# A decoder step on one core: order of the mixing block, place of the first squares, gates in steps, and an earlier verdict

## Chip, cores and metric
One core of one Trainium2 chip. The metric is device time in microseconds, from the start to the end of one execution; less is better.

## What is computed
One layer of a hybrid decoder for 256 prompt tokens and 8 single-token samples: a half-step SwiGLU, a mixing block, a second half-step SwiGLU, a final RMSNorm. The mixing block runs four mLSTM heads beside eight blocks of a gated short convolution.

```python
h = h + 0.5 * swiglu(rmsnorm(h, norm_ffn1), gate1, up1, down1)
h = h + mixing_block(rmsnorm(h, norm_mix), ...)
h = h + 0.5 * swiglu(rmsnorm(h, norm_ffn2), gate2, up2, down2)
y = rmsnorm(h, norm_final)
# in the mixing block
q, k, v, o, ig, fg, gb, gc, xc = split(h @ w_in)
ha = mlstm_chunkwise(q, k, v, logi, logf, C0, n0, m0)
ha = ha * rsqrt(mean(ha * ha) + EPS) * norm_mlstm * sigmoid(o)
yb = gb * (conv3(gc * xc) + conv_b)
yb = yb * rsqrt(mean(yb * yb, per group of 128) + EPS) * norm_conv
out = concat([ha, yb]) @ w_out
```

The new states C, n, m of every sample and of the prompt, and the last convolution inputs, are outputs too. D_MODEL is 2048, D_FF 5504, a head has 256 columns.

## The kernel before
Activations lie transposed: 16 blocks `h[kb]` of 128 features by 264 columns (256 prompt tokens and 8 samples), two blocks to a tile `hpair`. All weights are fp32 in memory and are used as two fp16 parts. `fetch` (L192) issues one transfer of up to 512 KB on SyncE's queue into `wraw`, ScalarE makes the high part `whi` (L178), VectorE the rest `wlo` (L186). `three` (L223) turns each 128x128 block into three matmuls: high weights by high and by low activations, low weights by high activations. A `product` (L228) runs such triples over all 16 input blocks into one of 8 PSUM banks, 48 matmuls. Six buffers of each weight tile exist; five tiles are kept ahead (`AHEAD`).

Each engine works through its instructions in the order in which the program issues them. `at(delta, fn)` (L209) puts a step on an agenda, and `tick` (L212) runs it when that many products later are reached; half ticks lie in the middle of a product. So the program's text fixes which steps stand between which weights on ScalarE and VectorE.

- **Opening.** `products4` (L249) runs the gate and up products of the first two FFN blocks, group by group of input blocks, while `ahead` (L435) loads `h`, cuts it into the parts `x` and squares it: even blocks on ScalarE, odd ones on GpSimd, which also adds all squares into `acc` (L382). Behind the four products `finish` (L384) lets TensorE sum `acc` over partitions (`column_sums`, L349), ScalarE and VectorE make 1/root from it, and then blocks 0 and 1 are scaled and activated (L409 to L422).
- **Mixing.** `MIX_ORDER` (L60) lists heads (6 products each), convolutions (3 each) and output gates (1 each). A head's steps follow over 13 ticks: scores, values, then for the samples four rounds of state loads, updates and outputs through GpSimd's queue, then the squares of its output (ScalarE, L869, tick 10.5), their addition `rs` (VectorE, L873, tick 11), the column sums (TensorE, tick 12) and the scaling (tick 13). `gate` (L957) runs at once: VectorE scales the product into `ta`, ScalarE takes the sigmoid `tb`, VectorE multiplies it into `ha`. The output products then read the convolution blocks `yb` first and the gated blocks `xa`, cut from `ha`, after them.
- **End.** The half-size arithmetic is watched: sums of each product go to `stat`, norms to `squares`. Behind the last output `judge` (L308) reduces them, TensorE sums the verdicts, and `bad` (L497) is loaded by every engine (L109). `tc.If` (L110) would run the whole step again in full fp32; it is not taken here, and every engine branches over that second program.

Of the kernel before, what the change touches and what calls it, by code (L numbers as in the profile page):

```python
# [8 lines left out]
F32 = mybir.dt.float32  # L9
# [3 lines left out]
ALU = mybir.AluOpType  # L13
# [46 lines left out]
MIX_ORDER = "h0 c0 c1 h1 c2 c3 h2 c4 c5 h3 c6 c7 o0 o1 o2 o3 o4 o5 o6 o7".split()  # L60
# [7 lines left out]
def weight_plan(a):  # L68
# [28 lines left out]
    for db in range(KB):  # L97
        add(("out", db), a["wout"][db], KB)
# [16 lines left out]
def step(ctx: ExitStack, tc: tile.TileContext, a: dict, bad=None):  # L115
# [6 lines left out]
    AHEAD = 5 if half_size else 2  # L122

# [16 lines left out]
    nc.gpsimd.dma_start(bg, a["bg"])  # L140
# [107 lines left out]

    def products4(x, ahead):  # L249
# [33 lines left out]
    if half_size:  # L283
        stat = const.tile([128, NSTAT], F32, name="stat")
        nc.gpsimd.memset(stat, 2.0 * SUMS[0])
        squares = const.tile([128, 8], F32, name="squares")
# [69 lines left out]
    class Norm:  # L356
# [5 lines left out]
        def block(self, kb, by_act=False):  # L362
            self.cut(kb)
            self.square(kb, by_act)
# [7 lines left out]
        def square(self, kb, by_act=False):  # L372
            new = self.acc is None
            sq = t264("acc", 1) if new else t264("sq")
            if by_act:
                nc.scalar.activation(sq, h[kb], AF.Square)  # L376
            else:
                nc.gpsimd.tensor_tensor(sq, h[kb], h[kb], op=ALU.mult)  # L378
# [4 lines left out]

        def finish(self, *rest, last=False):  # L384

            self.r = t264("rstd", 1)
            self.ssum = column_sums(self.acc, *rest)
# [5 lines left out]
    def ffn(layer, norm, done, start=None):  # L393
        with tc.tile_pool(name=f"act_{norm.tag}", bufs=1) as apool:
            first = True
            for half, blocks in enumerate(HALVES):
                act = {}
                for i, j in enumerate(blocks):
                    if start is not None and j < 2:
                        if j == 0:  # L400
                            ps4 = start()
                        pg, pu = ps4[2 * j : 2 * j + 2]
                    else:
                        pg = product((layer, "g", j), norm.x, range(KB))
                        pu = None
# [8 lines left out]
                    if pu is None:  # L414
                        pu = product((layer, "u", j), norm.x, range(KB))
# [19 lines left out]
    def ahead(part):  # L435
# [5 lines left out]
        for kb in range(k0, k0 + n):  # L441
            n1.block(kb, kb % 2 == 0)
# [8 lines left out]
        product=product, split=split, rsqrt=rsqrt, column_sums=column_sums, t264=t264,  # L451
        bank=bank, at=at, tick=tick, watch=watch, high=high, low=low, PART=PART, s3=s3,
# [6 lines left out]
    def done(kb):  # L459
# [4 lines left out]
        else:  # L464
            sq = t264("sq")
            nc.vector.tensor_tensor(sq, h[kb], h[kb], op=ALU.mult)
            nf.finish(sq, last=True)
            nc.scalar.activation(h[kb], h[kb], AF.Copy, scale=gain)
# [3 lines left out]
    def judge_early():  # L472
        early.append(len(stats))
        judge(stat[:, : early[0]], SUMS)

# [9 lines left out]

    if half_size:
        watch_norm(nf.ssum)
        judge(stat[:, early[0] : len(stats)], SUMS)
        judge(squares, SQUARES)
        ps = bank()[:1, :1]  # L490
        for i, v in enumerate(verdicts):
            nc.tensor.matmul(
                ps, v, ones[:, :1], start=(i == 0), stop=(i == len(verdicts) - 1)
            )
        some = const.tile([1, 1], F32, name="some")
        nc.vector.tensor_scalar(some, ps, 128.0 * len(verdicts) - 0.5, None, op0=ALU.is_lt)
        nc.vector.tensor_copy(bad, some)  # L497


def mix(tc, a, nm, n2, h, e):  # L500
# [6 lines left out]
    bank, at, tick = e["bank"], e["at"], e["tick"]  # L507
# [39 lines left out]
    nc.gpsimd.dma_start(m0, a["m0"])  # L547

    buf = mp.tile([128, 8, NS, 2], F32, name="buf")
    nc.gpsimd.dma_start(buf, a["conv0"])  # L550
# [25 lines left out]
    def gates_rows():  # L576
# [7 lines left out]
        nc.gpsimd.dma_start(drows, rows)  # L584
        nc.gpsimd.dma_start(a["m_p"], rows[:, 1, SEQ - 1 : SEQ])

    def gates_by_token():
# [17 lines left out]
        nc.gpsimd.dma_start(a["m_s"], ms)  # L605
# [480 lines left out]
```

## Time and profile before

| | us |
|---|---|
| median of 3 runs | 1876.56 (1875.29 to 1877.31) |
| the profiled execution | 1874.37 |
| its span, first to last instruction | 1872.5 |
| TensorE busy in the span | 1830.6 (98%), 16,107 instructions |
| VectorE, ScalarE, GpSimd busy | 1191.9, 859.6, 146.8 |

The mean granted TensorE clock over the span is 0.993. In the profile PE is TensorE's matmul, PEld its weight load, DVE is VectorE, ACT ScalarE, POOL GpSimd and SP SyncE; a q behind the name means the engine's instruction queue (branches, semaphores, loads of registers). A wait is put down to the instruction that released it last. Ends of matmuls are modelled, so the spacing of their starts tells more than their durations.

### The profile page before, as it was taken

What the parts mean: (1) busy time and instruction counts of PE and PEld (TensorE: products, weight loads), DVE (VectorE), ACT (ScalarE), POOL (GpSimd) and SP (SyncE); (2) the same over time, 40 slices, a digit from 0 to 9 for tenths busy, and PEclk for the clock granted to TensorE, in tenths of its full rate; (3) what the DMA queues carried; (4) which work ended last, traced back from release to release, by engine and by line L of the source; (5) the groups of instructions that cost most, each with busy time, mean ns of one, the idle gap of its engine ahead of it and who ended that gap; (6) DMA issues with size and microseconds to landing.
All of it is one profiled execution on the core that took longest, in us unless ns stands there. A gap on an engine that the chain in (4) does not pass through costs nothing.

```text
span 1872.5 us, 38560 instructions
## 1 busy us (share of the span) xinstructions
PE 1830.6 (98%) x16107; PEld 1586.8 (85%) x16107; DVE 1191.9 (64%) x1910; ACT 859.6 (46%) x1211; POOL 146.8 (8%) x219
## 2 busy tenths in 40 slices
PE   8999999999999999999999899999999999999994
PEld 6888888888888888888888688888888888888884
DVE  8666655466666557888888666666655456666453
ACT  6444443344444444656566645444443434444441
POOL 5000000000000211211211021000000000000110
PEclk9999999999999999999999999999999999999997
DMA  7666565656565555878778565656656656655551
GB/s 263 215 198 200 185 206 187 207 189 198 190 199 181 201 187 189 280 236 290 263 236 296 167 206 188 207 188 196 202 189 192 206 187 197 202 188 186 197 192 54
DMA packets 114714, 381.11 MB, mean 204 GB/s; under 512 B 14797, under 2 KB 19997, under 8 KB 114529
## 3 DMA queue, kind: packets, MB, share of 16 engines
q1 hardware_dynamic: 106048, 350.79, 57.4%
q0 software_dynamic: 8192, 27.57, 4.3%
q8 instruction: 128, 2.10, 0.4%
q14 instruction: 58, 0.47, 0.1%
q10 hardware_dynamic: 288, 0.19, 0.1%
HBM read 366.72 MB, written 11.78 MB: 202 GB/s over the span
## 4 chain that ended last, share of the span: by engine, by line
PE 82%; DVE 9%; issue 3%; ACT 2%; DMA 2%; POOL 0%; SPq 0%; DVEq 0%; ACTq 0%; POOLq 0%
PE ps L225 27%; PE ps L224 27%; PE ps L226 27%; DVE wlo L186 3%; DMA rb<-dr 1%; DVE cs L842 1%; ACT whi L178 1%; DVE jk L853 1%; ACT jk L861 1%; ACT L329 0%; DMA wraw<-in_w1gu 0%; DVE x L186 0%; DVE qkv L514 0%; DVE h L480 0%; DVE rs_q L338 0%
## 5 line engine op out<-in xcount | busy, mean ns | idle before, releaser
L186 DVE SCALAR_TENSOR_TENSOR wlo<-wraw,whi 128x1024 f16<-128x1024 f32 (+2 forms) x683 | 787.7, 1194 | 233.7 <-ACT whi L178 233.5
L226 PE MATMUL ps<-x,wlo 128*128 128x264 f16 x2752 | 759.6, 276 | 4.3 <-DVE wlo L186 4.3
L224 PE MATMUL ps<-x,whi 128*128 128x264 f16 x2752 | 759.6, 276 | 1.6 <-ACT whi L178 1.4
L225 PE MATMUL ps<-x,whi 128*128 128x264 f16 x2752 | 759.6, 276 | 0.0
L178 ACT ACTIVATE whi<-wraw 128x1024 f16<-128x1024 f32 (+2 forms) x683 | 664.9, 1016 | 165.5 <-PE ps L225 159.3
L226 PEld LDWEIGHTS <-wlo 128*128 128x128 f16 (+1 forms) x5296 | 518.6, 98 | 84.4 <-DVE wlo L186 6.5
L225 PEld LDWEIGHTS <-whi 128*128 128x128 f16 (+1 forms) x5296 | 518.6, 98 | 81.2 <-issue 1.8
L224 PEld LDWEIGHTS <-whi 128*128 128x128 f16 (+1 forms) x5296 | 518.6, 98 | 80.2 <-ACT whi L178 2.1
L224 PE MATMUL ps<-a,whi 128*128 128x264 f16 x1376 | 379.8, 276 | 0.0
L225 PE MATMUL ps<-a,whi 128*128 128x264 f16 x1376 | 379.8, 276 | 0.0
L226 PE MATMUL ps<-a,wlo 128*128 128x264 f16 x1376 | 379.8, 276 | 0.0
L224 PE MATMUL ps<-xm,whi 128*128 128x264 f16 (+1 forms) x912 | 252.3, 277 | 0.0
L225 PE MATMUL ps<-xm,whi 128*128 128x264 f16 (+1 forms) x912 | 252.3, 277 | 0.0
L226 PE MATMUL ps<-xm,wlo 128*128 128x264 f16 (+1 forms) x912 | 252.2, 276 | 0.0
L178 ACT ACTIVATE a<-tc 128x264 f16<-128x264 f32 x86 | 36.4, 423 | 295.0 <-DVE tc L418 292.6
L413 ACT ACTIVATE tb<-ta 128x264 f32<-128x264 f32 x86 | 36.3, 423 | 224.0 <-DVE ta L410 222.1
L425 DVE SCALAR_TENSOR_TENSOR h<-ps,h 128x264 f32<-128x264 f32 x64 | 27.7, 433 | 159.5 <-PE ps L226 159.5
L417 DVE TENSOR_TENSOR tc<-ps,rstd 128x264 f32<-128x264 f32 x86 | 37.1, 432 | 94.5 <-PE ps L226 94.5
L378 POOL TENSOR_TENSOR acc<-h 128x264 f32<-128x264 f32 x3 | 1.9, 626 | 1177.0 <-DVE stat L294 589.1
L410 DVE TENSOR_TENSOR ta<-ps,rstd 128x264 f32<-128x264 f32 x86 | 37.2, 432 | 60.4 <-PE ps L226 60.2
L186 DVE SCALAR_TENSOR_TENSOR a<-tc,a 128x264 f16<-128x264 f32 x86 | 37.3, 433 | 42.2 <-ACT a L178 42.2
L382 POOL TENSOR_TENSOR acc<-acc,sq 128x264 f32<-128x264 f32 x59 | 55.2, 936 | 6.4 <-ACT sq L376 1.8
(184 smaller groups left out, 864.8 us busy)
## 6 DMA issues: line engine op xcount, KB each, us to landing
wraw<-in_w2gu SPq DMA_DIRECT2D x172, 512.0 KB, 4.9
wraw<-in_w1gu SPq DMA_DIRECT2D x171, 512.0 KB, 4.8
wraw<-in_win SPq DMA_DIRECT2D x112, 512.0 KB, 5.5
wraw<-in_w1d SPq DMA_DIRECT2D x80, 448.0 KB, 4.1
wraw<-in_w2d SPq DMA_DIRECT2D x80, 448.0 KB, 4.0
wraw<-in_wout SPq DMA_DIRECT2D x32, 512.0 KB, 4.5
rb<-dr POOLq DMA_DIRECT2D x16, 513.0 KB, 10.2
wraw<-in_w1d SPq DMA_DIRECT2D x16, 512.0 KB, 4.4
```

The lines of the kernel that those rows point to most:

```text
L178: nc.scalar.activation(dst, src, AF.Copy, scale=scale)
L186: nc.vector.scalar_tensor_tensor(dst, src, scale, hi, op0=ALU.mult, op1=ALU.subtract)
L224: nc.tensor.matmul(ps, wh, xk[:, 0, :], start=first, stop=False)
L225: nc.tensor.matmul(ps, wh, xk[:, 1, :], start=False, stop=False)
L226: nc.tensor.matmul(ps, wl, xk[:, 0, :], start=False, stop=last)
L382: nc.gpsimd.tensor_tensor(self.acc, self.acc, sq, op=ALU.add)
L410: nc.vector.tensor_tensor(zg, pg, norm.r, op=ALU.mult)
L413: nc.scalar.activation(sg, zg, AF.Silu)
L417: nc.vector.tensor_tensor(zu, pu, norm.r, op=ALU.mult)
L425: nc.vector.scalar_tensor_tensor(h[db], ps, 0.5 / (sw * sa[layer]), h[db], op0=ALU.mult, op1=ALU.add)
L842: nc.vector.scalar_tensor_tensor(c[:, b, eb], rb[:, b, HD : 2 * HD], self.v[eb][:, col : col + 1], c[:, b, eb], op0=ALU.mult, op1=ALU.add,)
L853: nc.vector.tensor_tensor(jk, c, rb[:, :, :HD].unsqueeze(2).to_broadcast([128, 2, 2, HD]), op=ALU.mult)
```

## The change
- `MIX_ORDER`: head 1 follows one convolution, heads 2 and 3 two, and three convolutions stand behind the last head.
- The opening no longer squares. Behind the four products TensorE runs gate and up of block 2 as well; `square_pairs` lets ScalarE square two blocks of `h` at once, and GpSimd adds pairs, 528 columns at a time. The column sums then read both halves of the pair. Blocks 0, 1 and 2 are activated behind them.
- A gate becomes a class: sigmoid and multiplication are agenda steps one half to two ticks after its product, on a tile `zo` of its own; the cuts of `ha` are split in a high and a low step.
- `products2` runs the first two output products by turns, half of the input blocks each.
- The last norm is watched by a ScalarE activation that accumulates, the other norms are judged early, and the verdict is formed behind the sixth of the 16 last multiplications.
- In the full fp32 program (not run here) all transfers of GpSimd's queue go to SyncE's: `queue` stands for `nc.gpsimd` there and in the mixing block. In both programs `h[0]` is loaded on SyncE's queue, before the first weights.

```diff
-MIX_ORDER = "h0 c0 c1 h1 c2 c3 h2 c4 c5 h3 c6 c7 o0 o1 o2 o3 o4 o5 o6 o7".split()
+MIX_ORDER = "h0 c0 h1 c1 c2 h2 c3 c4 h3 c5 c6 c7 o0 o1 o2 o3 o4 o5 o6 o7".split()
...
+    half = KB // 2
+    for k0 in (0, half):
+        for db in range(2):
+            add(("out", db), a["wout"][db][:, k0 : k0 + half], half)
+    for db in range(2, KB):
         add(("out", db), a["wout"][db], KB)
...
+    queue = nc.gpsimd if half_size else nc.sync
...
-    nc.scalar.dma_start(h[0], a["xt"][:, 0, :])
     nc.scalar.dma_start(vecs, a["vecs"])
+    nc.sync.dma_start(h[0], a["xt"][:, 0, :])
...
+    def products2(keys, x, order):
+        ps = [bank()[:, :T] for _ in keys]
+        k = 0
+        while k < len(order):
+            tick()
+            for j, key in enumerate(keys):
...
+                if j == 0:
+                    tick(0.5)
+            k += n
+        return ps
...
+        def square_pairs(self, pool, pairs):
+            for i in pairs:
+                tag = f"sq{min(i, 1)}"
+                sq = pool.tile([128, 2, T], F32, tag=tag, name=tag, bufs=1 + 2 * min(i, 1))
+                nc.scalar.activation(sq, hpair[i], AF.Square)
+                if i == 0:
+                    self.acc = sq
+                else:
+                    nc.gpsimd.tensor_tensor(self.acc, self.acc, sq, op=ALU.add)
...
+                    if first and start is not None:
+                        ps4 = start()
+                        for n, ps in enumerate(ps4):
+                            early[n // 2, "gu"[n % 2]] = ps
+                        for step, pairs in ((0, (0, 1)), (1, (2, 3)), (1.5, (4, 5)), (2, (6, 7))):
+                            at(step, norm.square_pairs, apool, pairs)
+                        tick(0)
+                        for which in "gu":
+                            early[2, which] = product((layer, which, 2), norm.x, range(KB))
...
         for kb in range(k0, k0 + n):
-            n1.block(kb, kb % 2 == 0)
+            n1.cut(kb)
...
+            if half_size:
+                j = len(stats)
+                stats.append(j)
+                nc.scalar.activation(
+                    t264("ta"), nf.ssum, AF.Copy, scale=2.0**10, accum_out=stat[:, j : j + 1]
+                )
...
+        judge(squares, SQUARES)
...
+        if half_size and kb == 5:
+            judge_late()
...
+    class Gate:
+        def __init__(self, ob):
+            self.ob = ob
+            self.z = project(O + ob, tag="zo" if e["half_size"] else "ta")
+            steps = (1, 1.5, 2, 2) if ob == last[-1] else (1.5, 2, 2.5, 3)
+            at(steps[0], self.sigmoid)
+            at(steps[1], self.apply)
+            if ob in last:
+                at(steps[2], cut_high, ob)
+                at(steps[3], cut_low, ob)
...
-        for ob in tail:
-            gate(ob)
-            cut(ob)
...
+        for db, ps in enumerate(e["products2"]([("out", 0), ("out", 1)], x3, order)):
+            result(db, ps)
+        for db in range(2, KB):
+            result(db, product(("out", db), x3, order))
```

What the order of instructions becomes is shown at three places. First ScalarE's list in the opening, before: `x` is the high part of a block of `h`, `sq` its square.

```order
L178 ACTIVATE whi<-wraw 128x1024
L178 ACTIVATE x_423<-h_85,gains 128x264
L376 ACTIVATE sq<-h_85 128x264
L178 ACTIVATE x_429<-h_85,gains 128x264
L178 ACTIVATE whi<-wraw 128x1024 x6
L329 ACT_TABLE_LOAD
```

ScalarE's list at the same place now:

```order
L183 ACTIVATE whi<-wraw 128x1024 x6
L413 ACTIVATE sq_472<-h_78 128x528
L413 ACTIVATE sq_474<-h_79 128x528
L413 ACTIVATE sq_477<-h_80 128x528
L413 ACTIVATE sq_480<-h_81 128x528
L183 ACTIVATE whi<-wraw 128x1024
L413 ACTIVATE sq_514<-h_82 128x528
L413 ACTIVATE sq_517<-h_83 128x528
L413 ACTIVATE sq_544<-h_84 128x528
L413 ACTIVATE sq_547<-h_85 128x528
L183 ACTIVATE whi<-wraw 128x1024 x2
L356 ACT_TABLE_LOAD
```

All squares have moved behind the opening's weights, eight of 528 columns with one weight tile between them.

Second VectorE's list around the last head's addition of squares `rs`, before (`ha` is a gate's multiplication, `yc` a convolution's scaling):

```order
L945 SCALAR_TENSOR_TENSOR yc<-yc,vecs,rs 128x264
L514 TENSOR_TENSOR ta<-ps,rstd 128x264
L294 TENSOR_REDUCE stat<-ps 128x1
L962 SCALAR_TENSOR_TENSOR ha_8886<-ha_8886,vecs,tb 128x264
L873 TENSOR_TENSOR rs<-sq_13183 128x264
L186 SCALAR_TENSOR_TENSOR wlo<-wraw,whi 128x1024 x2
```

VectorE's list at the same place now:

```order
L997 SCALAR_TENSOR_TENSOR yc<-yc,vecs,rs 128x264
L566 TENSOR_TENSOR zo<-ps,rstd 128x264
L321 TENSOR_REDUCE stat<-ps 128x1
L925 TENSOR_TENSOR rs<-sq_12944 128x264
L984 TENSOR_TENSOR yc<-yc,tc 128x264
L191 SCALAR_TENSOR_TENSOR wlo<-wraw,whi 128x1024 x2
```

The multiplication of the gate whose product has just ended no longer stands ahead of the addition.

Third the end of the first program on VectorE, before (`h_78` to `h_85` are the pairs of output blocks):

```order
L480 TENSOR_TENSOR h_85<-h_85,rstd 128x264 x2
L304 TENSOR_REDUCE squares<-ps 128x1 x2
L312 TENSOR_SCALAR ok<-stat 128x9
L313 SCALAR_TENSOR_TENSOR ok<-stat,ok 128x9
L317 TENSOR_REDUCE verdict_23238<-ok 128x1
L312 TENSOR_SCALAR ok<-squares 128x8
L313 SCALAR_TENSOR_TENSOR ok<-squares,ok 128x8
L317 TENSOR_REDUCE verdict_23243<-ok 128x1
L496 TENSOR_SCALAR some<-ps 1x1
L497 CAST bad<-some 1x1
```

VectorE's end now:

```order
L543 TENSOR_TENSOR h_80<-h_80,rstd 128x264 x2
L339 TENSOR_SCALAR ok<-stat 128x10
L340 SCALAR_TENSOR_TENSOR ok<-stat,ok 128x10
L344 TENSOR_REDUCE verdict_23197<-ok 128x1
L536 TENSOR_SCALAR some<-ps 1x1
L537 CAST bad<-some 1x1
L543 TENSOR_TENSOR h_81<-h_81,rstd 128x264 x2
```

The flag has moved from behind the last multiplication to behind the sixth. At the same place, GpSimd's list ends so before (the instruction of L110 is the increment of its transfer queue's semaphores):

```order
L378 TENSOR_TENSOR sq<-h_23301 128x264
L382 TENSOR_TENSOR acc<-acc,sq 128x264
L110 UNCONDITIONAL_BRANCH
L110 ISA
L110 UNCONDITIONAL_BRANCH
L1066 ISA
```

GpSimd's list ends so now:

```order
L406 TENSOR_TENSOR acc<-acc,sq 128x264
L402 TENSOR_TENSOR sq<-h_23270 128x264
L406 TENSOR_TENSOR acc<-acc,sq 128x264
L114 UNCONDITIONAL_BRANCH x2
L1137 ISA
```

The increment between the two branches is gone.

## Rows read from the trace of the kernel before

**Rows 1.** Busy us (instructions) of each engine by stage, granted clock, DMA share and GB/s.
```profile
core 0: us, PE busy (x) PEld busy (x) DVE busy (x) ACT busy (x) POOL busy (x), PEclk, DMA share, GB/s
0.00:34.50 34.50, 27.55 (x212) 21.98 (x213) 28.78 (x36) 25.25 (x41) 25.61 (x31) 1.00 0.84 278
34.50:736.00 701.50, 701.50 (x6234) 610.27 (x6232) 423.59 (x638) 301.76 (x379) 25.44 (x36) 1.00 0.60 195
736.00:1070.00 334.00, 323.02 (x2755) 278.29 (x2753) 276.29 (x535) 200.01 (x374) 52.47 (x92) 0.99 0.75 253
```

**Rows 2.** Waits of PE: who waited for whom, us in total, times, longest us.
```profile
PE ps L492 <- DVE verdict L317: 9.0, 2, 8.6
PE ps L353 <- DVE rs L873: 8.6, 4, 6.3
PE ps L226 <- DVE wlo L186: 4.3, 8, 0.9
...
PE ps L224 <- ACT xa L178: 1.3, 1, 1.3
```

**Rows 3.** Timeline of PE in the opening: start, us, instruction, [idle before <-releaser].
```profile
6.34 0.29 PE L224 MATMUL ps<-x,whi 128*128 128x264 f16 x1 [1.44 <-ACT whi L178]
...
11.30 0.29 PE L226 MATMUL ps<-x,wlo 128*128 128x264 f16 x1 [0.86 <-DVE wlo L186]
...
33.91 0.61 PE L353 MATMUL ps<-acc,ones 128*128 128x264 f32 x2
34.35 0.28 PE L224 MATMUL ps<-x,whi 128*128 128x264 f16 x1
```

**Rows 4.** The chain that ended last, first 12 us: start, us, what.
```profile
2.88 6.03 DMA wraw<-in_w1gu
...
8.93 1.07 ACT whi L178
```

**Rows 5.** Groups by shape, DVE, 12 to 31 us: count, busy us, mean ns, idle before.
```profile
L186 DVE SCALAR_TENSOR_TENSOR x<-h,gains,x 128x264 f16<-128x264 f32 x12 | 11.2, 971 | 0.0
L186 DVE SCALAR_TENSOR_TENSOR wlo<-wraw,whi 128x1024 f16<-128x1024 f32 x6 | 9.9, 1643 | 0.0
```

**Rows 6.** The same groups from 36 to 1072 us.
```profile
L186 DVE SCALAR_TENSOR_TENSOR wlo<-wraw,whi 128x1024 f16<-128x1024 f32 x295 | 348.6, 1220 | 103.7 <-ACT whi L178 103.4 <-issue 0.2
...
L186 DVE SCALAR_TENSOR_TENSOR xm<-h,gains,xm 128x264 f16<-128x264 f32 x16 | 7.9, 494 | 9.3 <-ACT xm L178 9.3
```

**Rows 7.** Groups by shape, ACT, mixing stage.
```profile
L869 ACT ACTIVATE sq<-ha 128x528 f32<-128x528 f32 x4 | 2.5, 630 | 0.0
```

**Rows 8.** Groups by shape, POOL, 1740 to 1846 us.
```profile
L382 POOL TENSOR_TENSOR acc<-acc,sq 128x264 f32<-128x264 f32 x14 | 10.4, 744 | 1.1
```

**Rows 9.** Groups by shape, POOL, 12 to 31 us.
```profile
L382 POOL TENSOR_TENSOR acc<-acc,sq 128x264 f32<-128x264 f32 x12 | 14.5, 1211 | 0.9
```

**Rows 10.** Timeline of PE, late in the mixing stage.
```profile
1043.03 1.25 PE L353 MATMUL ps<-rs,ones 128*128 128x264 f32 x2 [6.29 <-DVE rs L873]
```

**Rows 11.** Busy time as in rows 1, 1043 to 1046.5 us.
```profile
1043.00:1046.50 3.50, 3.47 (x14) 2.28 (x15) 3.10 (x5) 1.33 (x3) 0.00 (x0) 0.50 0.22 73
```

**Rows 12.** Timeline of DVE at the same place.
```profile
1037.14 2.36 DVE L186 SCALAR_TENSOR_TENSOR wlo<-wraw,whi 128x1024 f16<-128x1024 f32 x2 [3.84 <-ACT whi L178]
```

**Rows 13.** Timeline of ACT at the same place.
```profile
1032.35 0.42 ACT L960 ACTIVATE tb<-ta 128x264 f32<-128x264 f32 x1 [3.02 <-DVE stat L294]
```

**Rows 14.** The chain that ended last, from 1846 us.
```profile
1850.69 5.54 DVE h L480 x16
...
1858.45 0.14 DVE bad L497
```

**Rows 15.** Instructions of L110: count, duration ns min/median/max, first and last start us.
```profile
L110 PEldq COMPARE_BRANCH  x1: 3764/3764/3764, 1859.2 to 1859.2; - x1
...
L110 POOLq INC_SWDGE_SEM  x1: 1716/1716/1716, 1863.7 to 1863.7; - x1
```

**Rows 16.** The same for L1066, the end of the program.
```profile
L1066 POOLq DRAIN  x3: 46/98/6271, 1865.4 to 1872.2; - x3
```

More of the change, by code (lines that the diff above doesn't have):

```diff
@@ L247, in product @@
         return ps
+    def products2(keys, x, order):
[4 more added lines that the diff above has]
+            for j, key in enumerate(keys):
+                while plan and len(ready) < AHEAD:
+                    fetch()
+                got, hi, lo, n = ready.pop(0)
+                assert got == key, (got, key)
+                for i in range(n):
+                    three(
+                        ps[j], hi[:, i, :], lo[:, i, :], x[order[k + i]], k + i == 0,
+                        k + i == len(order) - 1,
+                    )
+                fetch()
+                if j == 0:
+                    tick(0.5)
+            k += n
+        return ps
     def products4(x, ahead):
@@ L285, in step @@
         nc.gpsimd.memset(stat, 2.0 * SUMS[0])
-        squares = const.tile([128, 8], F32, name="squares")
+        squares = const.tile([128, 6], F32, name="squares")
     def watch(ps, rows=None):
@@ L394, in ffn, with gate_up @@
         with tc.tile_pool(name=f"act_{norm.tag}", bufs=1) as apool:
+            early = {}
+            def gate_up(j, which):
+                return early.pop((j, which), None) or product((layer, which, j), norm.x, range(KB))
             first = True
@@ L398, in ffn @@
                 for i, j in enumerate(blocks):
[L399 to L405, printed above, removed]
+                    if first and start is not None:
[7 more added lines that the diff above has]
+                            early[2, which] = product((layer, which, 2), norm.x, range(KB))
+                    pg = gate_up(j, "g")
                     if first:
@@ L413, in ffn @@
                     nc.scalar.activation(sg, zg, AF.Silu)
-                    if pu is None:
-                        pu = product((layer, "u", j), norm.x, range(KB))
+                    pu = gate_up(j, "u")
                     zu = t264("tc")
@@ L474, in judge_early, with judge_late @@
         judge(stat[:, : early[0]], SUMS)
+        judge(squares, SQUARES)
+    def judge_late():
+        judge(stat[:, early[0] : len(stats)], SUMS)
+        ps = bank()[:1, :1]
+        for i, v in enumerate(verdicts):
+            nc.tensor.matmul(
+                ps, v, ones[:, :1], start=(i == 0), stop=(i == len(verdicts) - 1)
+            )
+        some = const.tile([1, 1], F32, name="some")
+        nc.vector.tensor_scalar(some, ps, 128.0 * len(verdicts) - 0.5, None, op0=ALU.is_lt)
+        nc.vector.tensor_copy(bad, some)
     if half_size:
```

112 lines of the change are left out of this document (51 added, 61 removed).

## Prediction

> **What bounds the kernel now.** I read the busy time by stage first [rows 1]. From 34.5 to 736 us TensorE issues 6,234 instructions in 701.5 us without a break, 0.1125 us each. Only idle TensorE, or a lower clock, can be won: the instructions stay the same but for one pair. Idle time sits in three places: 6.95 us of the first 34.5 (27.55 busy), 11 us of the mixing stage (323.0 busy of 334), and all that follows the last product, some 24 us to the end of the span. The waits of TensorE by line [rows 2] name the owners: column sums of squares wait for VectorE's addition `rs` four times, 8.6 us, one of them 6.3; the first uses of `wlo` 4.3 us; the first `xa` 1.3 us; the verdict 9.0 us, which lies behind the last product and is read from the chain, not from TensorE. All sums are made against the profiled execution, 1874.37 us (span 1872.5 and 1.9 around it). It lies 2.2 us under the median of the runs, 1876.56, and at the end I add the difference to the median.
>
> **Start.** The first product runs at 6.34 us, the third group waits for `wlo` until 11.30, and the column sums follow the four opening products at 33.91 [rows 3]. The third group's weights land at 8.91 and ScalarE works on them for another 1.07 [rows 4]; that is a transfer, and the change leaves it nearly as it is (SyncE now issues h[0] first, so each weight transfer is issued one slot later, while `vecs` goes one slot earlier on ScalarE's queue). From there each group of 24 products is worth 24 x 0.1125 = 2.7 us of TensorE. VectorE needs two `x` and one `wlo`: 2 x 0.971 + 1.643 = 3.6 us less some overlap while GpSimd reads beside it [rows 5], but 2 x 0.494 + 1.220 = 2.2 us where GpSimd is mostly quiet [rows 6]. The change takes the squares out of this stretch, so VectorE falls under 2.7 and TensorE becomes the pace: from 11.30, 22 products of the third group and six groups of 24 are 166 x 0.1125 = 18.7 us, so 30.0 in place of 33.91, a gain of 3.9.
>
> The squares come back behind that. ScalarE squares pairs (0.63 us for 528 columns [rows 7]) once the last of the six listed `whi` is made, which needs a buffer that TensorE frees one group before the end: 27.3 + 1.07 = 28.4; two squares later, at 29.6, GpSimd adds the first pair. Seven additions of 528: one of 264 takes 0.744 alone [rows 8] and 1.211 beside a busy VectorE [rows 9], so 1.49 to 2.42 each plus 0.08 between them, 11.0 to 17.5 us, ready at 40.6 to 47.1. TensorE, which now runs the third block's gate and up products first (96 x 0.1125 = 10.8), stands there at 40.8. VectorE has only two `wlo` to do while ScalarE's queue is filled with squares, so I stay near the lower end and take 1 us of contention: ready at 41.6, a wait of 0.8. The second half of the pair costs the sums once more, 0.44 (34.35 - 33.91, [rows 3]). Before, the same point was at 33.91 + 0.44 + 10.8 = 45.15; now 40.8 + 0.8 + 0.88 = 42.5. **Start: -2.7** (-3.5 without a wait, +2.8 with 47.1).
> A rule speaks against this step. What the rows show is a partial slowdown: 1.211 against 0.744 on GpSimd, 1.643 against 1.220 on VectorE [rows 5, 6, 8, 9]. The Trainium skill (SBUF — State Buffer, Who interferes with whom) says that a VectorE instruction with two SBUF inputs and a GpSimd instruction that reads SBUF block each other fully. By that, each of the two `wlo` would add its whole 1.22 us to GpSimd's chain, the sums would be ready at 43.0, and the start would give 1.3 instead of 2.7. The durations say less than full blocking per instruction, so the sum above keeps the rows.
> Block 0, 1 and 2 are then activated in one run on VectorE and ScalarE. TensorE has four weight tiles in hand, 10.8 us; I take that as cover, at nothing. If it is too short, a wait of 1 to 2 us shows at the seventeenth tile.
>
> **Mixing stage.** The longest wait of all: the last head's column sums start at 1043.03 after 6.29 us of nothing [rows 10], and after it the granted clock is 0.50 (1.2 GHz) until 1046.5: 14 instructions in 3.47 us [rows 11], of which 12 would take 1.35 and the two of the sums 0.44 at 2.4 GHz, so 1.7 more. Together 8.0. The cause is a loop of queues: VectorE idles 3.84 us for a `whi` on ScalarE [rows 12], and ScalarE had idled 3.02 us for VectorE's gate input [rows 13], because each gate stands behind its own product on both engines. The change defers sigmoid and multiplication by half a product and more, and moves the last three convolutions between the head and the gates. What is late next is what the first three heads show: 8.6 - 6.3 = 2.3 us over three, about 0.8 each [rows 2]. So 8.0 becomes 0.9: -7.1. The first output products wait 1.3 us for `xa` (and VectorE's half of it); two products by turns put 5.4 us of convolution halves ahead of the gated half: -1.3. Against this, head 1 now starts 3 products after head 0, not 6; head 0's last squares share VectorE with head 1's sample vectors, where a lag of one product was already there; I add 1.0. **Mixing: -7.4** (from -11.8, no wait left, to -0.5, the long wait kept).
>
> **End.** After the last product VectorE makes 16 multiplications from 1850.69 in 5.54 us, two reductions of the norm and the verdicts follow, and `bad` stands at 1858.59 [rows 14]. Then every engine loads it, branches, and TensorE's queue takes 3.76 us for the branch alone; GpSimd follows with an increment of its queue's semaphores, 1.72 [rows 15], and a drain of 6.27 from 1865.4 [rows 16]. The change judges after six multiplications: 1850.69 + 6 x 0.346 = 1852.8, three judging operations, the small product, `some` and `bad` about 1.1: 1853.9. ScalarE, TensorE and GpSimd can branch 4.7 us earlier; the other ten multiplications end at 1857.4, so SyncE and VectorE come 1.2 earlier (the reductions are gone: one norm is watched by a ScalarE accumulation that stands beside Newton steps, and the squares are judged early). The branch path's second program no longer uses GpSimd's queue, and GpSimd's list loses the increment. The drain's price is not settled by one trace: if it only waits for the increment, both go, and the end hangs on VectorE and SyncE: -1.2, and -8.0 from the start of the increment to the drain's end, of which SyncE's own string of semaphores keeps 0.8: -8.4. If the drain costs 6.27 by itself, GpSimd's lead still gives 4.7 + 1.7 = -6.4. If it starts only when all engines are there, -1.2 - 1.7 = -2.9. I take the first, since the drain follows the increment directly. **End: -8.4** (-2.9 to -8.8).
>
> **Sum.** -2.7 - 7.4 - 8.4 = -18.5: 1855.9 for a profiled execution, 1858.0 at the median.
>
> **Rivals.**
> A. The drain stays. For: it is 3.7 times the increment and nothing in the trace says what it waits for. Against: the program's second half no longer has a use for the queue. +2.0 to +5.5: 1860.0 to 1863.5. Chance 0.20.
> B. GpSimd's additions run at their slow rate, and TensorE waits 6.3 us at the first column sums: +5.5, so 1863.5. For: [rows 9]. Against: VectorE has little to do there. Chance 0.12.
> C. The last head's wait stays as it is, since ScalarE's table loads for sigmoid and root still alternate there: +7.1, 1865.1. Chance 0.08.
> D. Slower than before: heads closer together make VectorE, busy 276 of 334 us in this stage [rows 1], the bound. Then each of the four column sums waits as the last one did, 8.0 with the clock: 32.0 against 8.0 + 2.3 now, +21.7 in place of -6.1. With start, end and the output products (-12.4) that is +9.3: 1885.9. It decides from a mean wait of (12.4 + 10.3) / 4 = 5.7 us a head. Against: only one pair of heads is closer, the other two keep 12 products. Chance 0.04.
>
> **How the numbers follow.** The forecast has 0.56. Predicted: 1858.0. Its own bounds are 1853 (every wait gone) to 1860; up to A, B and most of C the range runs to 1865.5. A measurement of this kernel can tell about 0.2% (3.7 us) from no change; all cases but D are faster by more. Faster 0.96, same 0.01, slower 0.03.
>
> **What would show it.** In the changed trace: column sums of the first norm near 42 us with a wait under 2 us; `x` on VectorE near 0.5 us before 30 us; no wait over 2 us at the four `rs` sums and no stretch at 0.50 clock in the mixing stage; no wait at the first `xa`; `bad` written near 4.5 us after the first final multiplication; no increment on GpSimd and no drain over 1 us. It is wrong if TensorE waits over 5 us in the opening, if any head's sum waits over 5 us, or if the end from the last product still takes over 20 us.

## The result and the profile after

The changed kernel takes 1859.18 us (median of four runs, 1858.52 to 1862.06); before takes 1876.06 beside it. The ratio is 0.991, 95% interval 0.9895 to 0.9925. The prediction was 1858.0, range 1852.5 to 1865.5. The gain is 0.9%, and the interval leaves no room for no change. The profiled execution takes 1858.52 us, its span is 1856.7.

Three marks on TensorE cut both executions into the prediction's three parts: the first transpose of the gates, the last norm's second column sum, and the end of the span. Timeline of TensorE before (start, us, instruction, [idle before]):

```profile
738.03 0.30 PE L590 MATMUL ps<-ident,gl 64*128 64x64 f32 x2 [0.75 <-DVE gl L579]
...
1847.98 0.71 PE L353 MATMUL ps<-sq,ones 128*128 128x264 f32 x2 [0.62 <-DVE sq L466]
```

The same marks after, with the first norm's column sums and the first head's:

```profile
42.85 1.16 PE L380 MATMUL ps<-sq,ones 128*128 128x264 f32 x4 [1.60 <-POOL sq L417]
...
736.78 0.31 PE L642 MATMUL ps<-ident,gl 64*128 64x64 f32 x2 [0.81 <-DVE gl L631]
...
819.35 0.71 PE L380 MATMUL ps<-rs,ones 128*128 128x264 f32 x2 [3.40 <-DVE rs L925]
...
1839.78 0.71 PE L380 MATMUL ps<-sq,ones 128*128 128x264 f32 x2 [0.62 <-DVE sq L511]
```

| part | before | after | difference | predicted |
|---|---|---|---|---|
| to the gates' transposes | 738.03 | 736.78 | -1.25 | -2.7 |
| from there to the last column sums | 1109.95 | 1103.00 | -6.95 | -7.4 |
| from there to the end of the span | 24.5 | 16.9 | -7.6 | -8.4 |

Together -15.8 in these two executions, -16.9 between the medians. TensorE's waits by line, after (as in [rows 2]):

```profile
PE ps L532 <- DVE verdict L344: 4.5, 1, 4.5
PE ps L380 <- DVE rs L925: 4.4, 2, 3.4
PE ps L380 <- POOL sq L417: 1.6, 1, 1.6
```

Busy time by stage, after (columns as in [rows 1]), and behind the first head's sums:

```profile
0.00:34.50 34.50, 30.28 (x246) 25.42 (x247) 24.49 (x39) 26.13 (x39) 4.59 (x11) 1.00 0.97 339
...
736.00:1070.00 334.00, 328.81 (x2816) 284.46 (x2817) 281.66 (x542) 205.29 (x380) 54.72 (x95) 0.99 0.77 260
...
819.30:823.70 4.40, 4.35 (x22) 3.42 (x23) 4.40 (x9) 2.85 (x4) 3.46 (x8) 0.61 0.60 160
```

Against [rows 1, 2]: TensorE is busy 30.28 of the first 34.5 us in place of 27.55, the waits for `rs` fall from 8.6 to 4.4, the one for `xa` is gone, the opening has a new one for GpSimd, and the mixing stage is 328.81 us busy in place of 323.02. The long wait has changed its owner. Before it was the last head's, 6.29 [rows 10]; that one is 1.01 now, and the first head's has grown from 0.48 to 3.40, with the granted clock at a mean of 0.61 in the 4.4 us behind it.

The end, instructions of the branch (L114) and of the program's end (L1137): count, duration ns min/median/max, first and last start:

```profile
L114 SPq EVENT_SEMAPHORE  x8: 17/17/17, 1853.9 to 1855.0; - x8
...
L114 POOLq COMPARE_BRANCH  x1: 45/45/45, 1846.4 to 1846.4; - x1
...
L114 POOLq EVENT_SEMAPHORE  x1: 17/17/17, 1846.8 to 1846.8; - x1
...
L114 SPq COMPARE_BRANCH  x1: 50/50/50, 1850.7 to 1850.7; - x1
...
L1137 SPq EVENT_SEMAPHORE  x14: 17/28/28, 1855.1 to 1856.7; - x14
...
L1137 POOLq DRAIN  x3: 50/98/6271, 1846.9 to 1856.5; - x3
```

The increment is gone, the drain of 6.27 us is not [rows 15, 16]. It runs from 1846.9 to 1853.2, while SyncE and VectorE still work on the output, and the last to arrive is SyncE: it issues the output's last transfers, branches at 1850.7, runs its next instruction at 1853.9, and its string of semaphores ends near 1855.8.

### The profile page after: what moved, and what is told of

It is laid out like the page before. It is cut to its first block, busy times and chain, and to the rows that moved or that the text cites. A ratio compares the mean times of both kernels' runs of the same rounds, so it can differ in the third digit from the quotient of the medians.

```text
span 1856.7 us, 38546 instructions
## 1 busy us (share of the span) xinstructions
PE 1829.2 (99%) x16109; PEld 1585.3 (85%) x16109; DVE 1184.3 (64%) x1908; ACT 863.3 (46%) x1213; POOL 133.8 (7%) x203
## 4 chain that ended last, share of the span: by engine, by line
PE 88%; DVE 5%; DMA 2%; issue 2%; ACT 1%; POOL 1%; SPq 0%; DVEq 0%; ACTq 0%; POOLq 0%
PE ps L229 29%; PE ps L230 29%; PE ps L231 29%; DVE wlo L191 2%; DMA wraw<-in_w1gu 1%; DMA rb<-dr 1%; ACT whi L183 1%; POOL sq L417 1%; DVE cs L894 0%; DVE jk L905 0%; PE ps L380 0%; ACT jk L913 0%; DVE h L543 0%; PE ps L821 0%; DMA dr<-r 0%
## 5 line engine op out<-in xcount | busy, mean ns | idle before, releaser
L321 DVE TENSOR_REDUCE stat<-ps 128x1 f32<-128x16 f32 x310 | 51.2, 165 | 0.0
```

The source lines that it names most:

```text
L321: nc.vector.tensor_reduce(stat[r, j : j + 1], ps[r, T - SEEN : T], axis=mybir.AxisListType.X, op=ALU.add, apply_absolute_value=True,)
```

## The experiments

One execution is a small sample here. Ten profiled executions with the new opening reach the gates' transposes between 736.8 and 739.0 us, mean 737.8; two with the old opening do at 738.0 and 738.5. Five profiled executions in which the middle part is the changed kernel's unaltered, with its opening too, take 1102.1 to 1103.2 us for it. The end took 15.8 to 17.1 us, mean 16.5, in the ten executions whose end is unaltered. The first head's wait is 1.75 to 3.81 us in the seven executions whose mixing block is unaltered. Times below are medians with the ratio to before; `after` is 0.991.

**u_order: the order of heads undone.** The gates stay in links, that is, sigmoid, multiplication and cuts stay separate agenda steps.

```diff
-MIX_ORDER = "h0 c0 h1 c1 c2 h2 c3 c4 h3 c5 c6 c7 ...
+MIX_ORDER = "h0 c0 c1 h1 c2 c3 h2 c4 c5 h3 c6 c7 ...
```

> The changed kernel with the order of before (two convolutions between heads, two behind the last), gates still in links. Theory: the links alone removed the last head's long wait, and the closer heads brought the new wait at head 0 (3.40 us and some 1.7 us at granted clock 0.50), because head 1's eleven sample-vector instructions now stand ahead of head 0's addition of squares on VectorE. Then head 0's sums wait about 0.5 us, no stretch at 0.50 clock is left there, the last head's sums wait under 1.5 us, and the time is 4.6 us less than the changed kernel's 1859.2: about 1854.6. Rival: the three convolutions behind the last head removed its wait. Then 6.3 us and 1.7 us of slow clock come back there while head 0 gains 4.6: about 1862.

1861.02 us, 0.992 (0.9906 to 0.9933). TensorE's waits in the mixing stage:

```profile
PE ps L380 <- DVE rs L925: 6.6, 3, 4.2
```

The middle part takes 1107.4, 4.4 more than the changed kernel's; this is the slowest of u_order's five executions, and by the medians the order is worth 1.8, with intervals that overlap. The last head waits 4.20 again, the first 1.90 and not the 0.5 that the theory named. So in this execution the links alone take 2.1 of the last head's 6.29 us and the new order, with three convolutions behind the last head, another 3.2; the rival was nearer, and the theory that the links had done it all fell.

**u_gates: immediate gates, new order.**

```diff
-            at(steps[0], self.sigmoid)
-            at(steps[1], self.apply)
+            self.sigmoid()
+            self.apply()
```

> The changed kernel with each gate's sigmoid and multiplication run directly behind its product, as before; the order of heads stays changed. Theory: the immediate gates alone make the last head's addition late, so its sums wait 5 to 6.3 us again and some 1.7 us follow at clock 0.50: 7 us more than 1859.2, about 1866. Rival: the three convolutions behind the last head suffice, its wait stays near 1.0 us, and the time stays within 1 us of 1859.2.

1865.56 us, 0.9944 (0.9931 to 0.9958), and 1108.5 for the middle part, 5.5 more. The time is what the theory gave, the place is not:

```profile
PE ps L380 <- DVE rs L925: 5.5, 4, 2.0
PE ps L230 <- DVE xa L191: 2.0, 1, 2.0
```

The last head waits 2.02, not 5 to 6.3. The first output products wait 2.0 for `xa` although they run by turns, so it is the links that removed that wait. VectorE's list at the last head shows `rs` behind a gate's multiplication that waits for ScalarE:

```profile
1022.76 0.49 DVE L1026 SCALAR_TENSOR_TENSOR ha<-ha,vecs,zo 128x264 f32<-128x264 f32 x1 [0.41 <-ACT zo L1021]
1023.17 0.43 DVE L925 TENSOR_TENSOR rs<-sq 128x264 f32<-128x264 f32 x1
```

The median is 6.4 over the changed kernel's, with intervals that don't overlap. One at a time, order and links undone cost 4.4 and 5.5 in the middle part; before, which has neither, takes 6.95 more. So the two overlap.

**u_start: the old place of the squares.**

```diff
             n1.cut(kb)
+            n1.square(kb, kb % 2 == 0)
...
-                        for step, pairs in ((0, (0, 1)), (1, (2, 3)), (1.5, (4, 5)), (2, (6, 7))):
-                            at(step, norm.square_pairs, apool, pairs)
-                        tick(0)
-                        for which in "gu":
-                            early[2, which] = product((layer, which, 2), norm.x, range(KB))
```

> The changed kernel with the opening's squares where they were: beside the first products, added 264 columns at a time on GpSimd, column sums behind the four products and block 2 after them; the loads keep the changed order. Theory: moving the squares is worth what the trace shows at the first product of block 3 (43.7 us against 45.15 before): 1.4 us more than the changed kernel, about 1860.6; x on VectorE takes about 0.95 us again and the column sums start near 33.9. Rival: the 1.4 us come from h[0] being loaded on SyncE's queue, since the first product starts 1.4 us earlier; then the time stays at 1859.2 and the sums start near 32.5. The prediction's own working would make it 2.7 us more, 1861.9.

1860.99 us, 0.9919 (0.9905 to 0.9932). VectorE in the opening (12 to 31 us, by shape) is as in [rows 5]:

```profile
L191 DVE SCALAR_TENSOR_TENSOR x<-h,gains,x 128x264 f16<-128x264 f32 x12 | 11.2, 972 | 0.0
L191 DVE SCALAR_TENSOR_TENSOR wlo<-wraw,whi 128x1024 f16<-128x1024 f32 x6 | 9.9, 1642 | 0.0
```

In the changed kernel the same groups take 488 and 1226 ns there. The rival, that the gain came from `h[0]` on SyncE's queue, fell: the first product starts at 5.19 in place of 6.34, but the third group waits for its `wlo` until 11.80 (before 11.30), and the column sums start at 34.41, not near 32.5. The transposes come at 738.5, 0.7 behind the mean of the new opening. (The middle part of this execution took 1104.8, though nothing in it is altered.) By the medians the move is worth 1.8 (1860.99 against 1859.18), with intervals that overlap. It gives up to some 2 us; the rows don't bear out 2.7.

**u_verdict: the verdict behind the last multiplication.**

```diff
-        if half_size and kb == 5:
+        if half_size and kb == KB - 1:
```

> The changed kernel with its verdict formed behind the last multiplication instead of the sixth. Theory: GpSimd's drain takes 6.27 us whatever precedes it and is hidden now only by the early verdict. The multiplications then end near 1849.0 in the span, the flag stands near 1850.2, the drain runs from 1851.4 to 1857.7 and ends last: 1.8 us more than the changed kernel, about 1861.0. Rival: the drain was long only for the increment before it. Then it is short here, SyncE's branch ends last as it does now, and the time rises by 0.5 us at most, about 1859.6.

1859.58 us, 0.9913 (0.9899 to 0.9926). GpSimd at its end (form as above):

```profile
L114 POOLq EVENT_SEMAPHORE  x1: 17/17/17, 1850.9 to 1850.9; - x1
...
L1137 POOLq DRAIN  x3: 50/98/6271, 1850.9 to 1857.8; - x3
```

The drain again takes 6271 ns with no increment ahead of it, and is now what ends last. The mechanism held; the price did not. The end is 17.8 us, 0.8 above the changed kernel's execution and 1.3 above the mean, so under 1.8. With the rest of the change in place the flag's place is worth about 1 us in these executions; the medians, 0.4 apart, don't show it. One cost of the early flag shows beside it. SyncE's transfers of the output, here and then in the changed kernel:

```profile
L547 SPq DMA_DIRECT2D out_yt<-h x7: 332/332/333, 1844.4 to 1848.6; - x7
...
DMA to landing us min/median/max: 2.1/2.2/2.2
```

```profile
L547 SPq DMA_DIRECT2D out_yt<-h x7: 332/383/1715, 1843.9 to 1850.2; - x7
...
DMA to landing us min/median/max: 2.1/4.0/4.7
```

With the flag behind them, here and in before, every issue takes 0.33 us and lands in at most 2.2. With the flag ahead of the last ones, in all twelve other executions, the longest issue takes 1.11 to 1.81 and the median landing 3.4 to 4.3.

**u_queue: the unused program's transfers back on GpSimd's queue.**

```diff
-    queue = nc.gpsimd if half_size else nc.sync
+    queue = nc.gpsimd
```

> The changed kernel with the transfers of the full fp32 program (not run) back on GpSimd's queue. Theory: GpSimd then needs 6.8 us from the flag to its drain as before (a branch of 4.0 us, four semaphores, the increment of 1.72) in place of 1.2, so the drain of 6.27 us ends near 1858.8 in the span and last: 3 us more than the changed kernel, about 1862. Rival, the prediction's case A: GpSimd's lead of the early verdict hides increment and drain, so nothing or at most 0.5 us is lost, 1859.5.

1860.55 us, 0.992 (0.9906 to 0.9933). GpSimd at the branch and the end:

```profile
L114 POOLq EVENT_SEMAPHORE  x5: 17/43/43, 1849.6 to 1849.9; - x5
...
L114 POOLq COMPARE_BRANCH  x1: 50/50/50, 1846.4 to 1846.4; - x1
...
L114 POOLq INC_SWDGE_SEM  x1: 1716/1716/1716, 1850.0 to 1850.0; - x1
...
L1137 POOLq DRAIN  x3: 46/98/6271, 1851.8 to 1858.6; - x3
```

From the branch to the next instruction GpSimd takes 3.2 us here and 0.4 in the changed kernel, and then the increment. The drain begins at 1851.8, 4.9 us later, and ends last; the end is 19.0 us, 2.1 more than the changed kernel's execution, 2.5 more than the mean. The theory's place of the drain's end held within a microsecond (1858.0 against 1858.8): part of what the early verdict buys is lost without the queue's move. The median lies 1.4 over the changed kernel's, between theory and rival, with intervals that overlap.

**f_end: the last five output transfers on ScalarE's queue.**

```diff
-            nc.sync.dma_start(a["yt"][:, kb - 1 : kb + 1, :], hpair[kb // 2])
+            out = nc.scalar if half_size and kb > 5 else nc.sync
+            out.dma_start(a["yt"][:, kb - 1 : kb + 1, :], hpair[kb // 2])
```

> The changed kernel with the last five transfers of the output issued on ScalarE's queue, not SyncE's. Theory: SyncE ends last because it can branch only behind the last of these transfers, needs 3.2 us for the branch and then its string of semaphores; ScalarE's branch took 2.5 us and it has no such string. SyncE is done with its string early but for the landing of the last transfers, and the end comes 1.3 to 2.6 us earlier: 1856.6 to 1857.9. Rival: the landing of the last transfer (about 1854.9 in the span) holds the end as well; then the time stays within 0.5 us of 1859.2.

1859.7 us, 0.9914 (0.99 to 0.9927): nothing gained.

```profile
L114 SPq EVENT_SEMAPHORE  x8: 17/17/17, 1851.6 to 1856.3; - x8
...
L114 SPq COMPARE_BRANCH  x1: 45/45/45, 1848.3 to 1848.3; - x1
...
L114 ACTq COMPARE_BRANCH  x1: 54/54/54, 1853.4 to 1853.4; - x1
L114 ACTq EVENT_SEMAPHORE  x1: 17/17/17, 1856.0 to 1856.0; - x1
```

Counted from the last column sums (1841.44 here), SyncE branches 4.1 us earlier than in the changed kernel, yet its eight semaphores, which wait for transfers, are spread over 4.7 us and end only 0.4 earlier, at 1856.3. ScalarE's five issues take 4.49 us, one of them 1.81, and a transfer lands up to 4.5 us after its issue; ScalarE itself branches only at 1853.4 and goes on at 1856.0. The rival held, and a second cause stood beside it.

**f_start: column sums in the middle of the next product.**

```diff
                             early[2, which] = product((layer, which, 2), norm.x, range(KB))
+                        at(1.5, norm.finish)
+                        early[3, "g"] = product((layer, "g", 3), norm.x, range(KB))
+                        first = False
```

> The changed kernel with the gate product of block 3 also run ahead of the activations, and the first norm's column sums put into the middle of it, 2.7 us later than now. Theory: GpSimd's chain of additions is ready at 43 to 43.7 us and the sums stand there at about 43.9, so the wait of 1.6 to 2.6 us and any slow stretch behind it vanish, and the time falls by about 2 us, to some 1857. Rival: with all eight banks in use, the up product of block 3 waits for a bank until the norm is there and block 0 is scaled, 2 us, and the time stays at 1859.

1858.66 us, 0.9909 (0.9894 to 0.9925). The sums run without a wait at 44.11, but:

```profile
49.29 0.27 PE L229 MATMUL ps<-x,whi 128*128 128x264 f16 x1 [1.32 <-DVE stat L321]
```

All eight banks are in use until VectorE scales block 0, and VectorE has four `wlo` until 47.4 ahead of that. The rival held: the wait of 1.6 became one of 1.3.

**f_add: a head's addition of squares half a tick earlier.** VectorE ahead of the first head's sums, in the changed kernel:

```profile
813.33 2.36 DVE L191 SCALAR_TENSOR_TENSOR wlo<-wraw,whi 128x1024 f16<-128x1024 f32 x2 [2.35 <-ACT whi L183]
815.61 0.41 DVE L846 COPY r<-ps 8x256 f32<-8x256 f32 x1
...
818.40 0.13 DVE L865 COPY r<-sm 8x1 f32<-8x1 f32 x1
...
818.88 0.41 DVE L925 TENSOR_TENSOR rs<-sq 128x264 f32<-128x264 f32 x1
```

The squares are made by 814.8; between `wlo` and `rs` stand the eleven sample-vector instructions of head 1 (2.9 us) and the scaling of a product.

```diff
-            at(11, self.add_squares)
+            at(10.5, self.add_squares)
```

> The changed kernel with one number altered: a head adds its squares half a tick earlier, in the same half tick as ScalarE's squaring, so head 0's addition stands ahead of head 1's eleven sample-vector instructions (2.9 us) on VectorE. Theory: their place ahead of it is the cause of head 0's wait. Then that wait falls from 3.40 us to about 0.5, no stretch at clock 0.50 follows it, the last head's wait of 1.0 falls to 0.5 or less, and the time falls by some 5 us to about 1854. Rival: VectorE is late there whatever the order, since it waits 2.35 us for whi just before; the wait moves to the next user of VectorE (scores or the next product's bank), and the time falls by 1 us at most.

1856.33 us, 0.989 (0.9875 to 0.9905). The first head's wait falls to 0.83, and the last one's is gone. In the three executions with this edit and this order (f_decay and f_best below are the others) the first head waits 0.83, 0.34 and not at all, against 1.75 to 3.81 in the seven without the edit, so the instructions ahead of `rs` were the cause. But ScalarE and TensorE now show this while head 1 is under way, TensorE at a convolution's sums:

```profile
859.51 1.33 ACT L885 ACTIVATE cs<-cs,rb 128x512 f32<-128x512 f32 x2 [3.48 <-DMA rb<-dr]
...
865.01 0.71 PE L380 MATMUL ps<-sq,ones 128*128 128x264 f32 x2 [2.51 <-ACT sq L988]
```

The middle part takes 1103.3, as in the changed kernel. So in this execution, the slowest of f_add's four, the theory held for the wait and the rival for the sum: the wait moved. The median, 2.9 under the changed kernel's, lies between the two. It is the lowest of all kernels, but its interval overlaps with the changed kernel's. That it beats the changed kernel stays open.

**f_shift: the same, with the short distance between heads 1 and 2.**

```diff
-MIX_ORDER = "h0 c0 h1 c1 c2 h2 c3 c4 h3 ...
+MIX_ORDER = "h0 c0 c1 h1 c2 h2 c3 c4 h3 ...
```

> The kernel with the earlier addition of squares, and one convolution moved: two between heads 0 and 1, one between heads 1 and 2. Theory: with the addition ahead of the next head's sample vectors the distance of one convolution no longer makes a wait, wherever it stands; each head's sums wait under 1.2 us, and the time is within 1.5 us of 1856.3. Rival: one convolution between two heads is too close in itself; head 1's sums then wait 2.5 to 4 us in place of head 0's.

1858.2 us, 0.9908 (0.9893 to 0.9923). TensorE's waits in the mixing stage:

```profile
PE ps L380 <- ACT sq L988: 2.5, 2, 1.8
...
PE ps L380 <- DVE rs L925: 0.7, 2, 0.5
```

No head's sums wait more than 0.51, so one convolution between two heads is not too close in itself; the 2.5 us for `sq` are two convolutions' sums. The theory held for the waits and missed the time by a little (1.9 over f_add's median, 1.5 allowed). The middle part is 1100.7, 2.3 less than the changed kernel's, while the opening of this execution was 2.3 later; the medians don't tell the two apart.

**f_decay and f_best: the decay of the sample states half a tick later, alone and with f_start's edit.** Both stand on f_add.

```diff
-                at(3.5 + 1.5 * n, self.sample_decay, n)
+                at(4 + 1.5 * n, self.sample_decay, n)
```

> The kernel with the earlier addition of squares (1856.3), and ScalarE's decay of the sample states half a tick later in each of the four rounds. There ScalarE waited 3.48 us for the rows rb, which make a way through DRAM, with the next weights' high parts queued behind it, and TensorE then waited 2.51 us at 862.5. Theory: what the earlier addition won came back in part as this wait. Then it goes, no wait over 1.5 us is left in the mixing stage, and the time falls by 1 to 2.5 us, to about 1854.5. Rival: the wait at 862.5 was of that one execution; the time stays at 1856.3 or rises, since the later decay delays the update behind it.

> The same two edits with the column sums of the first norm in the middle of block 3's gate product, which alone gave 0.5 us. Theory: the parts lie in different stages and add: about 1854. Rival: the parts overlap, 1856.

1863.88 us, 0.9938 (0.9924 to 0.9951), and 1864.01, 0.9942 (0.9928 to 0.9955): both slower than the changed kernel. In f_decay, VectorE and ScalarE at head 1:

```profile
851.11 1.68 DVE L894 SCALAR_TENSOR_TENSOR cs<-rb,qkv,cs 128x256 f32<-128x256 f32 x4 [1.96 <-ACT cs L885]
...
858.22 0.42 ACT L183 ACTIVATE yb<-yc 128x264 f16<-128x264 f32 x1 [4.27 <-DVE yc L997]
```

The wait for `rb` is gone there, and the two engines wait for each other instead; two convolutions' sums wait 3.1 us each. The theory fell, and with it the parts can't be added in f_best. Whether `rb`'s way through memory caused f_add's wait is not settled by it.

**after_again: the changed kernel once more**, beside the last three.

> The changed kernel once more, unaltered, as the measure for the three kernels beside it on the same chip. If head 0's wait belongs to the order of instructions, it shows again at 1.7 to 3.8 us; the time is 1859.2, give or take 1.

1858.21 us, 0.9909 (0.9894 to 0.9925). The first head waits 2.33.

## Why the prediction was right, step by step

**Start: the sign held, the size did not.** VectorE's relief came as worked out (`x` 488 ns, `wlo` 1226; predicted 494 and 1220), and TensorE became the pace, from 11.61 on and not from 11.30. The step that failed is the time at which the squares begin. It was put at 28.4 by a buffer that TensorE frees; ScalarE's list shows another cause:

```profile
27.98 1.06 ACT L183 ACTIVATE whi<-wraw 128x1024 f16<-128x1024 f32 x1 [0.21 <-DMA wraw<-in_w1gu]
29.27 1.06 ACT L183 ACTIVATE whi<-wraw 128x1024 f16<-128x1024 f32 x1 [0.23 <-DMA wraw<-in_w1gu]
30.23 2.23 ACT L413 ACTIVATE sq<-h 128x528 f32<-128x528 f32 x4
```

Each `whi` waits for its transfer, one per 1.28 us, so the squares begin at 30.2 and the first addition at 31.47, not 29.6. (The last of these transfers was issued at 22.8, when VectorE had just finished with its buffer, and took 6.3 us.) The chain of seven additions took 11.3 us, against 11.0 plus 1 of contention; it came out near because two errors cancel, a cheaper addition (1.31 against 1.49) and dearer meetings with `wlo`. Rows of GpSimd, then of VectorE:

```profile
31.47 1.31 POOL L417 TENSOR_TENSOR sq<-sq,sq 128x528 f32<-128x528 f32 x1 [28.54 <-ACT sq L413]
...
32.86 1.31 POOL L417 TENSOR_TENSOR sq<-sq,sq 128x528 f32<-128x528 f32 x1
34.24 2.16 POOL L417 TENSOR_TENSOR sq<-sq,sq 128x528 f32<-128x528 f32 x1
...
40.64 2.16 POOL L417 TENSOR_TENSOR sq<-sq,sq 128x528 f32<-128x528 f32 x1
...
33.44 1.81 DVE L191 SCALAR_TENSOR_TENSOR wlo<-wraw,whi 128x1024 f16<-128x1024 f32 x1 [1.85 <-ACT whi L183]
...
39.45 2.19 DVE L191 SCALAR_TENSOR_TENSOR wlo<-wraw,whi 128x1024 f16<-128x1024 f32 x1 [4.20 <-ACT whi L183]
```

Two of the seven additions, each begun beside a `wlo`, take 2.16 in place of 1.31, 1.7 us in all where 1.0 was taken; the three `wlo` take 1.81, 2.19 and 2.31 in place of 1.22.
The starts and ends show how. The addition of 32.86 keeps its 1.31 and ends at 34.17; the `wlo` that began beside it ends 1.08 behind that, at 35.25; the addition of 34.24 ends 1.16 behind the `wlo`. From 39.25 to 43.88 addition, `wlo`, addition and `wlo` follow each other likewise, each ending 1.07 to 1.16 behind the one before. So whichever starts second makes hardly any headway until the first is done, and a duration counts that wait as well. In all twelve executions with the squares in their new place the durations of these meetings are the same within 0.02 us.
The Trainium skill (SBUF — State Buffer, Who interferes with whom) says that a VectorE instruction with two SBUF inputs contends with a GpSimd instruction that reads SBUF, and calls the port pair that they share an exclusive lock. These rows agree with it. The prediction set its rule aside because the mean durations showed a partial slowdown; that reading was wrong, since a mean mixes additions that met a `wlo` with others that did not. Its estimate by the rule, sums ready at 43.0 and a start of 1.3, came near to what was measured in part by chance: it began the squares 1.8 us too early, and added a whole `wlo` twice where 0.85 us each were lost.
The sums are ready at 42.8 (predicted 41.6), and the wait is 1.6, in the other executions with this opening 1.1 to 2.6. In three of these ten, the mean granted clock from 43 to 50 us is then 0.76 in place of 1.00, which the sum had no term for. On the mean of the executions the start gives 0.4, in the pair shown 1.25. The four weight tiles were cover enough: TensorE does not wait while blocks 0 to 2 are activated.

**Mixing: near in its sum by luck, through errors that cancel.** The last head's 8.0 became 1.0 (predicted 0.9), the `xa` wait went, as predicted. Two terms were mis-sized. The waits of the two middle heads, 1.26 and 0.60, which the sum kept, are gone in this execution (in u_queue the third head waits 2.40, while the first waits 1.75, and the middle part is no longer for it). The closer heads, priced at 1.0, cost 2.9 of wait at head 0 and, by the 22 instructions in 4.4 us, 1.7 of clock. By the rows that makes 7.0 + 1.9 + 1.5 (`xa`, both parts) - 4.6 = 5.8 of the 6.95; some of the rest is the 0.2 us of each wait that the modelled end of the matmul before it covers (four waits fewer, 0.7 us as an estimate); what is left is not accounted for. The prediction named the pair of heads but took a product's lag as harmless; f_add shows that it was eleven instructions standing half a tick ahead of `rs` in one queue. The cause it gave for the old wait, the gates behind their own products, is part of the story: of the last head's 6.29 us the links alone remove 2.1 (u_order), the order alone 4.3 (u_gates), both together 5.3.

**End: near in size by luck, wrong in its reason.** The likeliest case was that increment and drain both vanish. Rival A was true in that the drain costs 6.27 by itself: it does in all 14 profiled executions, with and without the increment. But its price of +2.0 to +5.5 was wrong, since the sum missed a term. Before, GpSimd needed 6.8 us from the flag (1858.59) to the drain (1865.41), now 1.2 (1845.69 to 1846.92): besides the 1.72 of the increment and the semaphores ahead of it, 3.5 us between branch and next instruction have gone, and u_queue brings 2.8 of them back.
The Trainium skill (Runtime: NRT & Kernel Launch, Instruction fetch mechanics) says that a taken branch out of the prefetched window waits for a fetch. GpSimd's 0.4 us with its transfers moved away and 3.2 with them fit that, though no view here shows the fetch itself; the page gives no time.
So the drain ends at 1853.2, and SyncE, which the prediction had put 1.2 earlier and at the end together with VectorE, is last alone. Counted from the last column sums, it branches only 0.6 us earlier than before (10.9 against 11.5), since its transfers are slowed as u_verdict shows; with the late flag of u_verdict it branches at 10.3. The sum had no term for that. VectorE is not last: its load and branch run at 1845.7 to 1846.4, while its last ten multiplications run until 1849.1. The term of judging was right: the flag stands 3.2 us behind the first multiplication, as worked out (1853.9 less 1850.69); the 4.5 in the list of signs belonged to no term.

**Sum.** For a profiled execution the sum gave 1855.9, and 1858.52 was measured. The median came nearer, 1.2 us off, because the execution of before lay 2.2 us under the median that the sum was carried to and this one lies 0.7 under its own; that part is luck too. Of the signs, three failed: a head's sums wait 3.40, a stretch at a mean clock of 0.61 follows, and the drain takes over 1 us. None of the signs of being wrong came.

**Rivals.** B's long wait in the opening did not come (1.1 to 2.6, not 6.3). C's last-head wait did not stay, but u_order shows that without the new order more than half of it would have stayed. D, VectorE as the bound, did not come; a trace of it may be visible in f_add and f_decay, where a wait removed comes back further on in the queues of VectorE and ScalarE.

## What to carry to other kernels

When a chain of short steps runs through in-order queues, list what stands ahead of the step that TensorE waits for, in the same half tick, before counting distances in products. Price an engine's end by its own list from the flag to its last instruction, branch and all, and expect that removing one engine's tail gives only the distance to the next one's. A stretch priced by buffers needs a look at its transfers first. A mean duration can hide that two engines take turns: lay their rows side by side before choosing between a slowdown and a lock.

## What the runs showed of the hardware

- GpSimd's drain at the end of the program takes 6271 ns in all 14 profiled executions, with and without the increment ahead of it.
- From a taken branch to the next instruction GpSimd takes 0.4 to 0.5 us with its transfers in the skipped program on another queue, and 4.0 (before) and 3.2 (u_queue) with them on its own; over all executions ScalarE takes 2.5 to 3.9, SyncE 3.2 to 4.2, TensorE 3.7 to 4.5.
- A GpSimd addition of 528 columns (1.31 us alone) and VectorE's `wlo` (1.22) take turns: the one that starts second ends 1.07 to 1.16 us behind the first, in the five meetings from 32.86 to 43.88 us of the changed kernel.
- A transfer's issue, usually 0.33 to 0.44 us at the end, took 1.72 on SyncE (changed kernel) and 1.81 on ScalarE (f_end) while other engines were between branch and next instruction, and the output's transfers landed up to 4.8 us after their issue (u_queue); in before and u_verdict, with no engine at the branch yet, 0.33 and 2.2.
